# Output projection of a decoder trunk: a longer lag for the residual's squares and stores, and transfers of computed data issued from GpSimd's queue

## The chip, the cores and the metric

The kernel runs on one core of a Trainium2 chip. The metric is the device time of one execution in microseconds (us), lower is better. The core has four engines with instruction queues of their own, each worked off in order: TensorE (PE, matrix products into PSUM), VectorE (DVE, here V), ScalarE (ACT, here S) and GpSimd (POOL, here G). A fifth, SyncE (SP, `nc.sync`), issues transfers only. Transfers between the core's SBUF and device memory are issued from a queue, here SP's or POOL's, and run on 16 DMA engines. An instruction that waits holds up everything behind it in its queue.

## The reference: what is computed

One decoder layer over 2048 tokens of width 1024, all in float32. Two token mixers (a gated delta rule and a linear recurrence, four heads each) make `mix`. The part around the change is

```python
mix_out = jnp.einsum('btc,cd->btd', mix, w_out[i])
h = h + rms_norm(mix_out, post_mix_norm[i])

u = jnp.einsum('btd,df->btf', rms_norm(h, pre_mlp_norm[i]), w_mlp_up[i])
y = jnp.einsum('btf,fd->btd', jnp.square(jax.nn.relu(u)), w_mlp_down[i])
h = h + rms_norm(y, post_mlp_norm[i])
```

Behind it a per-layer embedding, projected and gated by a sigmoid, is added.

## The kernel before

**Stages.** Activations are held transposed: 128 channels on the partitions, 512 tokens (a block, `q` = 0 to 3) along a row. A 1024-wide activation of a block is eight tiles of 128x512 (256 KB each). The stages run one behind the other: input projection and token mixers (to about 1136 us), output projection (to about 1326 us), MLP up and down, gate. Every float32 operand of a product is split into a high part (ScalarE, L164 or L217) and a low part (VectorE, L165 or L218, which subtracts the high part and so follows ScalarE's half), and a product is three matmuls: high by high, high by low, low by high. PE needs a weight tile's high part first and its low part two matmuls later.

**Output projection (L1335 to L1382).** The loop goes over `j` = 0 to 31, that is four blocks `q` by eight output tiles `d`; one `(q, d)` is 24 matmuls, `mmo`. Its weights `w_out` are loaded raw (512 KB, L338) and split for the first three blocks, and reloaded as stored split (1 MB, L185) for the fourth, two or three tiles ahead. Three split weight buffers and two raw ones exist. ScalarE copies the result from PSUM (`yo`, L1374) and squares it (`sq_o`, L233); VectorE sums the squares (`acc_o`, L234).

For blocks 0 and 1 the sum goes through a norm (`rstd_steps`: split `hl`, product with ones on PE, L1156 and L1157, then logarithm, exponential and a correction on ScalarE and VectorE, to `r_o`). `residual_by_dma` then takes the eight tiles: VectorE scales one (L1210), POOL issues a transfer that adds x onto it in place (L1211), and some steps later its square goes into a second sum (`sq_h`, `acc_h`) and the tile is stored (`h1d`, L1214). From `acc_h` a second norm gives `rn`, the scale of the MLP's input.

For blocks 2 and 3 the unscaled tile is stored (`yod`, L1378) from a pool of two buffers, `stg`: the copy of tile d waits until the store of tile d - 2 has landed. Their residual is made later, within the MLP (`passed`).

**The MLP's operands.** The MLP's products are Strassen-like: seven products of sums of quarters. For the first half (blocks 0 and 1) `early_operands` reloads block 0's `h1d` as `be` (L1269), and `up_operands` reloads block 1's as `b` (L1288), in four steps of two tiles; VectorE scales them by `rn`, forms differences (L1293 to L1304) and splits them into `t`. Four quarter tiles of `w_up` are loaded into the raw buffers (`u_raw`, L1350), combined and split into `w_u`. PE's first products `u` (L1125) use `t` and `w_u`.

**What sets the order.** PE's order is as written. A clock ticks once every eight matmuls (`mm`, `tick`), and `later` puts the steps of a generator at tick offsets, here `OUT_STEPS`: one step of the residual per tick from offset 7 on, the second norm's product at offset 26. Within that, a planner decides how the instructions of ScalarE, VectorE, POOL and SP stand in their queues, and all of them run in that order. `pair` and `squares` rotate the buffers of the squares.

Of the kernel before, what the change touches and what calls it, by code (L numbers as in the profile page):

```python
# [43 lines left out]
N_CONST = C_MASK + len(LEVELS)  # L44


OUT_STEPS = (1, 5) + tuple(range(7, 18)) + (18, 26)
MLP_STEPS = (1, 5) + tuple(range(7, 25, 2))
AMID_STEPS = (1, 5) + tuple(range(12, 39, 3))

# [38 lines left out]
def trunk(ctx, tc, x, xT, pT, vecs, w_in, w_ab, gdn_a_log, gdn_dt_bias, w_out, w_up, w_down,  # L89
          w_ple, w_gate, consts, out):  # L90
    nc = tc.nc
    V, S, G, PE = nc.vector, nc.scalar, nc.gpsimd, nc.tensor
# [32 lines left out]
    def col(r):  # L125
        return cols[:, r : r + 1]
# [95 lines left out]
    def squares(acc, src, k, name, eng=V):  # L222

        if acc is None:
            acc = st.tile([P, QT], F32, tag="acc", name=f"acc_{name}", bufs=3)
            S.activation(acc, src, AF.Square)
        else:
            turns[0] += 1
            if pair[0] and turns[0] % 2:
                sq = st.tile([P, QT], F32, tag="late", name=f"sq_{name}_{k}")  # L230
            else:
                sq = st.tile([P, QT], F32, tag="sq", name=f"sq_{name}_{k}", bufs=1)
            S.activation(sq, src, AF.Square)  # L233
            eng.tensor_tensor(acc, acc, sq, ALU.add)  # L234
        return acc
# [23 lines left out]
    h1d = [[dr.tile([P, QT], F32, name=f"h1d{q}_{k}") for k in range(KD)] for q in range(NQ)]  # L259
# [63 lines left out]
    def mix_operands(q):  # L323
        xin[q] = []
        for k in range(KD):
            t = next_pool().tile([P, 2, QT], F32R, tag="ring", name=f"mixT{q}_{k}")
            nc.sync.dma_start(plain(t), mixd[q][k])
            split_in_place(t)
            xin[q].append(t)
            yield  # L330
# [4 lines left out]
    def stage_out(j):  # L335
        if j < len(order) and order[j][0] < RAW:
            raw = wp.tile([P, KD, P], F32, tag="raw", name=f"raw_out{j}", bufs=2)
            nc.sync.dma_start(raw, w_out[order[j][1]])  # L338
            staged_out[j] = raw
# [77 lines left out]
    with mixers as mctx:  # L417
# [515 lines left out]
        for q in range(NQ):  # L933
            works.append((f"ab{q}", "ab", w_ab, q, None, None, None, None))
            for h in range(4):
                g, b = {}, {}
# [97 lines left out]
        with tc.manual_schedule(engines={mybir.EngineType.SP}):  # L1034
# [26 lines left out]
            qs = (2, 3)  # L1061
# [25 lines left out]
            while clock[0] <= last or len(held) < 2 or 1 in ready:  # L1087
                if fill:
                    q, d = fill.pop(0)
# [26 lines left out]
    def later(gen, offsets):  # L1116
        for o in offsets:
            agenda.setdefault(clock[0] + o, []).append(gen)
# [21 lines left out]
    def ytile(name):  # L1140
        return f2.tile([P, QT], F32, tag="y", name=name, bufs=16)
# [61 lines left out]

    def residual_by_dma(q, ys, rsb, skip, gain, dst, name, sums):

        total, lag = None, 3
        for d in range(KD + lag):
            yield
            if d < KD:
                V.scalar_tensor_tensor(ys[d], ys[d], col(gain + d), rsb, ALU.mult, ALU.mult)  # L1210
                G.dma_start(ys[d], skip(d), accum_op=ALU.add)  # L1211
            if d >= lag:
                total = squares(total, ys[d - lag], d - lag, f"{sums}{q}")
                nc.sync.dma_start(dst[d - lag], ys[d - lag])  # L1214
        yield
        return total

# [26 lines left out]
    yod = {q: [dr.tile([P, QT], F32, name=f"yod{q}_{d}") for d in range(KD)] for q in (2, 3)}  # L1244

    def run(gen):
        for _ in gen:
            pass
# [4 lines left out]
    def moving(half, n, k, raw):  # L1253
        x = next_pool().tile([P, 2, QT], F32R, tag="ring", name=f"t{n}_{half}_{k}")
        split(x, V, raw)
        tops[half][n].append(x)

    def start_operands(half):
        tops[half] = {n: [] for n in ("11", "3", "1", "2", "21", "4", "22")}
# [3 lines left out]
    def early_operands():  # L1263

        start_operands(0)
        for k in range(KD // 2):
            for n, kk in (("11", k), ("21", k + KD // 2)):
                b = first_b[kk] = ytile(f"be_{kk}")
                nc.sync.dma_start(b, h1d[0][kk])  # L1269
                V.scalar_tensor_tensor(b, b, col(R_PREMLP + kk), h1_r[0], ALU.mult, ALU.mult)  # L1270
                moving(0, n, k, b)
                yield

    def up_operands(half, rsb):

        qs = (2 * half, 2 * half + 1)
        early = half in tops
        if not early:
            start_operands(half)
        for k in range(KD // 2):  # L1280
            n = f"{half}_{k}"
            b11, b21, b12, b22, t3, t2, t4 = (once(lambda i=i: ytile(f"b{i}_{n}")) for i in range(7))
            if early:
                b11, b21 = (lambda k=k: first_b[k]), (lambda k=k: first_b[k + KD // 2])
            for b, s, kk in ((b12, 1, k), (b22, 1, k + KD // 2), (b11, 0, k), (b21, 0, k + KD // 2)):
                if early and s == 0:
                    continue
                nc.sync.dma_start(b(), h1d[qs[s]][kk])  # L1288
                V.scalar_tensor_tensor(b(), b(), col(R_PREMLP + kk), rsb[s], ALU.mult, ALU.mult)
            yield  # L1290
            if not early:
                moving(half, "11", k, b11())
            V.tensor_tensor(t3(), b22(), b12(), ALU.subtract)  # L1293
            V.tensor_tensor(b12(), b12(), b11(), ALU.subtract)
            yield
            moving(half, "3", k, t3())
            moving(half, "1", k, b12())
            yield
            V.tensor_tensor(t2(), b22(), b12(), ALU.subtract)
            moving(half, "2", k, t2())  # L1300
            if not early:
                moving(half, "21", k, b21())
            yield
            V.tensor_tensor(t4(), b21(), t2(), ALU.subtract)  # L1304
            moving(half, "4", k, t4())
            moving(half, "22", k, b22())
            yield

    def once(make):
        kept = []  # L1310

        def get():
            if not kept:
                kept.append(make())
            return kept[0]

        return get
# [18 lines left out]
    for j, (q, d) in enumerate(order):  # L1336
        if d == 0:
            ys, acc = [], None
            if q < 2:
                later(mix_operands(q + 1), range(2, 18, 2))  # L1340
            if q == 1:
                later(mix_operands(3), range(17, 25))
        ready_out(j + 2)
        stage_out(j + 3)
        if j == len(order) - 5:
            u_raw = [wp.tile([P, 2, QT], F32, tag="raw", name=f"u_raw{i}", bufs=2) for i in range(2)]
            a1, a2 = w_up[0], w_up[FF // P // 2]
            for t, i, src in ((u_raw[0], 0, a1[:, : KD // 2]), (u_raw[1], 1, a1[:, KD // 2 :]),
                              (u_raw[0], 1, a2[:, : KD // 2]), (u_raw[1], 0, a2[:, KD // 2 :])):
                nc.sync.dma_start(t[:, i].rearrange("p (k n) -> p k n", n=P), src)  # L1350
        if j == len(order) - 2:
            two_blocks(("11", u_raw[0][:, 0]), ("12", u_raw[1][:, 1]))
        if j == len(order) - 1:
            (a11, a21), (s1, s4) = ((t[:, 0], t[:, 1]) for t in u_raw)
            b22 = two_blocks(("22", s1), None)
            V.tensor_tensor(s1, s1, a21, ALU.add)
            V.tensor_tensor(a21, a11, a21, ALU.subtract)
            V.tensor_tensor(a11, s1, a11, ALU.subtract)
            V.tensor_tensor(s4, s4, a11, ALU.subtract)
            u_block("3", b22, a21)  # L1360
        if (q, d) == (2, 1):
            early = early_operands()
            later(early, range(0, 2 * KD, 2))
        if prep is None and h1_r[1] is not None:
            run(early)
            prep = up_operands(0, h1_r)
            later(prep, range(0, 24, 1))
        if j in held:
            ps = held.pop(j)
        else:  # L1370
            ps = bank(f"mmo_{q}_{d}", pp)
            product(ps, columns(ready.pop(j)), xin[q])
        y = ytile(f"yo{q}_{d}") if q < 2 else tp.tile([P, QT], F32, tag="stg", name=f"yo{q}_{d}")
        S.activation(y, ps, AF.Copy)  # L1374
        acc = squares(acc, ps, d, f"o{q}")
        ys.append(y)
        if q >= 2:
            nc.sync.dma_start(yod[q][d], y)  # L1378
        if d == KD - 1 and q < 2:
            later(normed(q, ys, acc, lambda d, q=q: xT[blk(d), tok(q)], R_POSTMIX, h1d[q], "o", "h"), OUT_STEPS)  # L1380
        elif d == KD - 1:
            later(rstd_steps(acc, 1.0 / D, EPS, f"o{q}", row_of(o_r, q), po, wait=True), OUT_STEPS[:2] + (9,))  # L1382
    u_block("2", two_blocks(("1", s1), None), a11)
# [353 lines left out]
    for half in range(2):  # L1737
        qs = (2 * half, 2 * half + 1)
# [75 lines left out]
```

## Time and profile before

| | us |
|---|---|
| median of three runs | 2731.33 (2723.95 to 2732.11) |
| profiled execution | 2734.69 |
| its span | 2732.5 |
| PE busy | 2661.9 (97%) |
| VectorE busy | 2037.9 (75%) |
| ScalarE busy | 1467.6 (54%) |
| POOL busy | 116.7 (4%) |

A group of the page gives line, engine, operation, output and inputs, the count, then busy time and the mean of one in ns, then the idle time just ahead of it and who ended it. A row of the timeline gives the start, the length, the engine, line and operation, and the count where several follow each other; what stands in brackets is the idle time ahead of it and its releaser. `SPq` is SP's queue. A row of the waits gives who waited for whom, in total, how often, and the longest. The time of a transfer to its landing counts from its issue to the event that says that all its data are there.

### The profile page before, as it was taken

The page shows a single profiled execution, that of the slowest core. Times are in us where ns is not written, and L with a number is a line of the kernel's source. Part 1 is how long each engine was busy: PE and PEld are TensorE (multiplying, and loading weights), DVE is VectorE, ACT ScalarE, POOL GpSimd, SP SyncE. Part 2 cuts the span into 40 slices and gives each one's busy share as a digit, 9 for nine tenths or more (in the row PEclk, how much of TensorE's full clock was granted, in tenths as well). Part 3 has the DMA queues.
Part 4 walks back from the last instruction along what each step waited for, and adds up shares of the span by engine and source line. Part 5 has one row for each costly group of instructions (what it writes and reads, how often), then busy time and mean ns, then how long its engine had stood idle before and what let it go on. Part 6 is the DMA issues. An engine that isn't in the chain of part 4 may idle for free.

```text
span 2732.5 us, 38474 instructions
## 1 busy us (share of the span) xinstructions
PE 2661.9 (97%) x12745; PEld 2214.0 (81%) x12745; DVE 2037.9 (75%) x4228; ACT 1467.6 (54%) x2944; POOL 116.7 (4%) x120
## 2 busy tenths in 40 slices
PE   7999999999999999998999999999999999999999
PEld 5788788888888887776788888888888888888887
DVE  6788877787778777566889867767787765567776
ACT  6665555465546445566655646555554445465431
POOL 0000000000000000011000000001000000001000
PEclk9999999999999999999999999999999999999999
DMA  7777777667665665788566547667554446687664
GB/s 249 259 265 227 238 253 248 219 214 260 214 215 205 216 210 176 246 266 264 173 232 224 189 153 256 207 207 241 169 204 146 151 167 214 189 257 239 217 209 138
DMA packets 268742, 589.24 MB, mean 216 GB/s; under 512 B 55658, under 2 KB 60232, under 8 KB 249344
## 3 DMA queue, kind: packets, MB, share of 16 engines
q1 hardware_dynamic: 266240, 582.59, 64.3%
q0 software_dynamic: 2304, 4.20, 0.9%
q8 instruction: 101, 1.65, 0.3%
q14 instruction: 97, 0.79, 0.1%
HBM read 419.75 MB, written 166.92 MB: 215 GB/s over the span
## 4 chain that ended last, share of the span: by engine, by line
PE 51%; DMA 4%; issue 3%; DVE 2%; ACT 1%; POOL 1%; SPq 0%; DVEq 0%; POOLq 0%; ACTq 0%
PE u L1125 22%; PE d L1125 21%; PE mmg L1125 6%; PE mmo L1125 1%; DMA raw_out<-in_w_out_dram 1%; DMA yo<-in_xT_dram 1%; DMA b<-h1d 0%; POOL acc_y L234 0%; DMA mixT<-mixd 0%; DMA rd_g<-m_g 0%; DMA w_out<-cache_out 0%; PE mme L191 0%; DMA raw_pT<-in_pT_dram 0%; DVE t L165 0%; DMA m_g<-sd_g 0%
## 5 line engine op out<-in xcount | busy, mean ns | idle before, releaser
L1054 PE MATMUL mm<-xt,w 128*128 128x512 f32 x3072 | 784.9, 401 | 2.1 <-ACT zt_zg L559 2.1
L1054 PEld LDWEIGHTS mm<-xt,w 128*128 128x128 f32 x3072 | 554.3, 189 | 102.6 <-ACT zt_zg L559 2.5
L1125 PE MATMUL d<-db,da 128*128 128x512 f32 x2688 | 610.6, 389 | 0.2 <-DVE db L218 0.2
L1125 PE MATMUL u<-t,wu 128*128 128x512 f32 x2604 | 591.1, 389 | 0.0
L1125 PEld LDWEIGHTS d<-db,da 128*128 128x128 f32 x2688 | 504.5, 188 | 105.7 <-DVE db L218 1.0
L1125 PEld LDWEIGHTS u<-t,wu 128*128 128x128 f32 x2604 | 488.9, 188 | 101.4
L218 DVE TENSOR_TENSOR db<-db 128x512 fp32r<-128x512 f32 x224 | 160.0, 714 | 69.2 <-ACT db L217 68.2
L1477 DVE TENSOR_TENSOR u<-u,u 128x512 f32<-128x512 f32 x224 | 150.4, 683 | 57.2 <-PE u L1125 55.7
L1125 PE MATMUL mmo<-mixT,w_out 128*128 128x512 f32 x720 | 173.4, 400 | 14.8 <-ACT w_out L164 7.7
L217 ACT ACTIVATE db<-db 128x512 fp32r<-128x512 f32 x224 | 140.9, 629 | 74.8 <-DMA db<-hid 70.7
L1125 PEld LDWEIGHTS mmo<-mixT,w_out 128*128 128x128 f32 x720 | 137.5, 193 | 49.5 <-ACT w_out L164 10.4
L1125 PE MATMUL mmg<-h2T,wg 128*128 128x512 f32 (+1 forms) x792 | 174.8, 383 | 0.0
L1125 PEld LDWEIGHTS mmg<-h2T,wg 128*128 128x128 f32 x792 | 145.6, 188 | 29.0
L1520 ACT ACTIVATE u<-u 128x512 f32<-128x512 f32 x128 | 80.8, 631 | 161.3 <-DVE u L1477 160.8
L165 DVE TENSOR_TENSOR da<-da 128x512 fp32r<-128x512 f32 x128 | 93.6, 731 | 83.3 <-ACT da L164 83.0
L164 ACT ACTIVATE da<-da 128x512 fp32r<-128x512 f32 x128 | 80.5, 629 | 128.5 <-DMA da<-sumd 105.7
L164 ACT ACTIVATE wu<-a 128x512 fp32r<-128x512 f32 x124 | 75.0, 623 | 48.0 <-DMA a<-in_w_up_dram 46.1
L680 DVE TENSOR_TENSOR pr_g<-xs_g,sys_g 128x16 f32<-128x16 f32 (+14 forms) x240 | 94.4, 393 | 5.6
L165 DVE TENSOR_TENSOR wu<-a,wu 128x512 fp32r<-128x512 f32 x124 | 85.7, 693 | 10.5 <-ACT wu L164 10.5
L234 POOL TENSOR_TENSOR acc_y<-acc_y,sq_y 128x512 f32<-128x512 f32 x28 | 38.6, 1380 | 1253.7 <-ACT sq_y L233 1253.7
L1521 ACT ACTIVATE u<-u 128x512 f32<-128x512 f32 x128 | 80.5, 629 | 3.1
L165 DVE TENSOR_TENSOR da<-dr,da 128x512 fp32r<-128x512 f32 x96 | 66.3, 691 | 18.0 <-ACT da L164 16.0
(383 smaller groups left out, 3790.9 us busy)
## 6 DMA issues: line engine op xcount, KB each, us to landing
w<-cache_in SPq DMA_DIRECT2D x96, 1024.0 KB
db<-hid SPq DMA_DIRECT2D x224, 256.0 KB
cache_in<-w SPq DMA_DIRECT2D x32, 1024.0 KB
hid<-u SPq DMA_DIRECT2D x128, 256.0 KB
da<-sumd SPq DMA_DIRECT2D x128, 256.0 KB
a<-in_w_up_dram SPq DMA_DIRECT2D x124, 256.0 KB
hid<-ht SPq DMA_DIRECT2D x96, 256.0 KB
dr<-in_w_down_dram SPq DMA_DIRECT2D x96, 256.0 KB
```

The lines of the kernel that those rows point to most:

```text
L164: S.activation(t[:, 0], raw, AF.Copy)
L165: eng.tensor_tensor(t[:, 1], raw, t[:, 0], ALU.subtract)
L217: S.activation(t[:, 0], plain(t), AF.Copy)
L218: V.tensor_tensor(t[:, 1], plain(t), t[:, 0], ALU.subtract)
L234: eng.tensor_tensor(acc, acc, sq, ALU.add)
L680: V.tensor_tensor(pr[:, :, :, 0:i], xs[:, None, :, 0:i].broadcast_to([P, 2, GC, i]), sys[:, 0:i, i : i + 2].rearrange("p j two -> p two j" ...
L1054: PE.matmul(ps, *terms[i], start=i == 0, stop=i == nt - 1)
L1125: PE.matmul(ps, a, b, start=start, stop=stop)
L1477: V.tensor_tensor(c[new], c[old], ps, ALU.add)
L1520: S.activation(c[k], c[k], AF.Relu)
L1521: S.activation(c[k], c[k], AF.Square)
```

## The change

The lag between a tile's scaling and its square and store in `residual_by_dma` goes from three steps to five, and `OUT_STEPS` gets two more steps in the row so that the generator ends at the same tick (26); the split of the summed squares moves from offset 18 to 20. The stores `h1d` of blocks 0 and 1, the stores `yod` of blocks 2 and 3, the reloads `be`, and the loads `b` of the MLP's first half are issued from POOL's queue instead of SP's. These are the transfers of the stage that wait for computed data. Loads of weights and of `mixT` stay on SP.

```diff
-OUT_STEPS = (1, 5) + tuple(range(7, 18)) + (18, 26)
+OUT_STEPS = (1, 5) + tuple(range(7, 20)) + (20, 26)
...
     def residual_by_dma(q, ys, rsb, skip, gain, dst, name, sums):
 
-        total, lag = None, 3
+        total, lag = None, 5
         for d in range(KD + lag):
             yield
             if d < KD:
                 V.scalar_tensor_tensor(ys[d], ys[d], col(gain + d), rsb, ALU.mult, ALU.mult)
                 G.dma_start(ys[d], skip(d), accum_op=ALU.add)
             if d >= lag:
                 total = squares(total, ys[d - lag], d - lag, f"{sums}{q}")
-                nc.sync.dma_start(dst[d - lag], ys[d - lag])
+                G.dma_start(dst[d - lag], ys[d - lag])
...
                 b = first_b[kk] = ytile(f"be_{kk}")
-                nc.sync.dma_start(b, h1d[0][kk])
+                G.dma_start(b, h1d[0][kk])
...
-                nc.sync.dma_start(b(), h1d[qs[s]][kk])
+                (nc.sync if half else G).dma_start(b(), h1d[qs[s]][kk])
...
         if q >= 2:
-            nc.sync.dma_start(yod[q][d], y)
+            G.dma_start(yod[q][d], y)
```

## The prediction

> **What bounds the kernel now.** The page comes first: its span, and the groups of TensorE by line.
>
> ```profile
> span 2732.5 us, 38474 instructions
> ...
> L1125 PE MATMUL u<-t,wu 128*128 128x512 f32 x2604 | 591.1, 389 | 0.0
> ...
> L1125 PE MATMUL mmo<-mixT,w_out 128*128 128x512 f32 x720 | 173.4, 400 | 14.8 <-ACT w_out L164 7.7
> ```
>
> PE sets the time. In the MLP's first product (`u`) it never idles; in the output projection (`mmo`), the stage of the change, it idles 14.8 us, mostly for weights that ScalarE and VectorE split. A microsecond saved here counts only if the next stage takes it over. The timeline of PE shows where it stops (a bracket is the idle time before the row, and who ended it).
>
> ```profile
> 1186.88 34.62 PE L1125 MATMUL mmo<-mixT,w_out 128*128 128x512 f32 x152
> 1222.31 0.73 PE L1125 MATMUL mmo<-mixT,w_out 128*128 128x512 f32 x2 [0.82 <-ACT w_out L164]
> 1223.57 3.47 PE L1125 MATMUL mmo<-mixT,w_out 128*128 128x512 f32 x14 [0.53 <-DVE w_out L165]
> ...
> 1248.35 11.83 PE L1125 MATMUL mmo<-mixT,w_out 128*128 128x512 f32 x48 [0.53 <-DVE w_out L165]
> 1261.14 5.29 PE L1125 MATMUL mmo<-mixT,w_out 128*128 128x512 f32 x22 [0.96 <-DVE w_out L165]
> 1268.71 0.79 PE L1125 MATMUL mmo<-mixT,w_out 128*128 128x512 f32 x2 [2.29 <-ACT w_out L164]
> 1271.70 7.34 PE L1125 MATMUL mmo<-mixT,w_out 128*128 128x512 f32 x22 [2.19 <-DVE w_out L165]
> 1281.12 3.96 PE L1125 MATMUL mmo<-mixT,w_out 128*128 128x512 f32 x16 [2.08 <-DMA w_out<-cache_out]
> ...
> 1291.27 34.62 PE L1125 MATMUL mmo<-mixT,w_out 128*128 128x512 f32 x152
> ...
> 1331.91 0.73 PE L1125 MATMUL u<-t,w_u 128*128 128x512 f32 x2 [0.58 <-ACT w_u L164]
> 1333.05 2.11 PE L1125 MATMUL u<-t,w_u 128*128 128x512 f32 x8 [0.41 <-DVE w_u L165]
> ```
>
> Undisturbed, matmuls follow each other by (34.62 - 0.39) / 151 = 0.227 us (row 1291.27). By that pace the first block would reach the third row at 1221.8; it starts at 1223.57: 1.8 us lost. In the same way 1.9 are lost ahead of 1261.14, 2.6 ahead of 1268.71, 2.5 ahead of 1271.70 and 4.4 ahead of 1281.12: 13.2 us in all, which is the most that this change can win here. The last two rows matter as much: behind the stage PE already waits, if briefly, for VectorE and ScalarE. PE has no lead there to give away.
>
> Why are the weights late? The waits of the stretch 1185 to 1335, of the engines and of SP's queue:
>
> ```profile
> ACT sq_h L233 <- DMA yo<-in_xT_dram: 16.0, 11, 2.5
> ```
> ```profile
> SPq L1214 <- DMA yo<-in_xT_dram: 34.3, 13, 7.0
> ```
>
> Both wait for the accumulating transfer that adds x onto the scaled tile (L1211). ScalarE's squares come three ticks (of eight matmuls, 1.8 us) behind the scaling, the transfer is often not in, and the split of the weights stands behind the square. SP's store waits likewise, with weight loads queued behind it. ScalarE's timeline:
>
> ```profile
> 1220.20 0.63 ACT L233 ACTIVATE sq_h<-yo 128x512 f32<-128x512 f32 x1 [2.44 <-DMA yo<-in_xT_dram]
> ...
> 1221.21 1.05 ACT L164 ACTIVATE w_out<-raw_out 128x1024 fp32r<-128x1024 f32 x1
> ...
> 1255.08 0.63 ACT L226 ACTIVATE acc_h<-yo 128x512 f32<-128x512 f32 x1 [3.67 <-DMA yo<-in_xT_dram]
> ...
> 1262.12 0.63 ACT L233 ACTIVATE sq_h<-yo 128x512 f32<-128x512 f32 x1 [2.10 <-DMA yo<-in_xT_dram]
> 1264.44 0.63 ACT L233 ACTIVATE sq_h<-yo 128x512 f32<-128x512 f32 x1 [1.68 <-DMA yo<-in_xT_dram]
> ...
> 1267.62 1.04 ACT L164 ACTIVATE w_out<-raw_out 128x1024 fp32r<-128x1024 f32 x1
> ...
> 1274.02 0.63 ACT L233 ACTIVATE sq_h<-yo 128x512 f32<-128x512 f32 x1 [1.72 <-DMA yo<-in_xT_dram]
> ...
> 1282.47 0.60 ACT L1374 ACTIVATE yo<-mmo 128x512 f32<-128x512 f32 x1 [4.33 <-DMA yod<-yo]
> ...
> 1285.58 0.63 ACT L164 ACTIVATE hl_o<-acc_o 128x512 fp32r<-128x512 f32 x1 [2.02 <-PE nrm_h L1157]
> ```
>
> **The change, part by part.** No arithmetic is added or removed, and PE's order stays as it is. Two more ticks (3.6 us) put squares and stores later; `OUT_STEPS` is stretched so that the sum's split comes two ticks later and the norm at the same tick 26. 48 issues (16 stores `h1d`, 16 stores `yod`, 8 loads `be`, 8 loads `b`) leave SP for POOL, which now has only the 16 adds there. POOL's rows, and VectorE's and SP's that the steps need:
>
> ```profile
> 1251.39 0.88 POOL L1211 DMA_DIRECT2D yo<-in_xT_dram  x1 [37.84 <-DVE yo L1210]
> ...
> 1255.06 2.68 POOL L1211 DMA_DIRECT2D yo<-in_xT_dram  x3 [1.52 <-DVE yo L1210]
> 1262.64 0.88 POOL L1211 DMA_DIRECT2D yo<-in_xT_dram  x1 [4.90 <-DVE yo L1210]
> ...
> 1267.41 0.88 POOL L1211 DMA_DIRECT2D yo<-in_xT_dram  x1 [2.10 <-DVE yo L1210]
> ```
> ```profile
> L1211 POOL DMA_DIRECT2D yo<-in_xT_dram x16: 875/875/1355, 1198.3 to 1267.4; - x16
> ...
> DMA to landing us min/median/max: 3.7/6.4/10.6
> ```
> ```profile
> 1270.43 1.22 DVE L165 TENSOR_TENSOR w_out<-raw_out,w_out 128x1024 fp32r<-128x1024 f32 x1
> ...
> 1304.89 1.42 DVE L1289 SCALAR_TENSOR_TENSOR b<-b,cols,rn 128x512 f32<-128x512 f32 x2 [0.82 <-DMA b<-h1d]
> ...
> 1315.80 0.75 DVE L1289 SCALAR_TENSOR_TENSOR b<-b,cols,rn 128x512 f32<-128x512 f32 x1 [0.65 <-DMA b<-h1d]
> ...
> 1322.30 1.42 DVE L1289 SCALAR_TENSOR_TENSOR b<-b,cols,rn 128x512 f32<-128x512 f32 x2
> ```
> ```profile
> 1273.27 0.47 SPq L185 DMA_DIRECT2D w_out<-cache_out  x1
> ...
> 1274.37 0.40 SPq L1378 DMA_DIRECT2D yod<-yo  x1
> ...
> 1300.20 0.92 SPq L1288 DMA_DIRECT2D b<-h1d  x2
> ...
> 1319.60 0.88 SPq L1288 DMA_DIRECT2D b<-h1d  x2
> ```
>
> *First block (q = 0).* ScalarE's order in the changed program has the split of 1221.21 ahead of the last two squares, behind the sixth, which can run at about 1216.6 as its data land. The split starts near 1218, before PE asks: the 1.8 us go. VectorE's queue, which takes over the waits in between, comes out 1.4 us earlier. I take 1.4.
>
> *Second block (q = 1).* The changed POOL queue reads:
>
> ```
> add0 add1 store0 add2 add3 add4 yod3 store1 store2 store3 add5 add6 yod4 add7 store4 .. store7 yod5 b b yod6 yod7
> ```
>
> A store waits until its add has landed, and the adds behind it wait too. Store0 goes at 1255.08 (add0 has landed), so adds 2 to 4 go 0.9 later than now. Store2 waits for add2: now 1255.06 to 1262.12, 7.1 us; so 1263.0. Store3 waits for add3: 8.5 from its issue to 1264.44; so 1265.4. Add5 then goes at 1266.2 in place of 1262.64, add7 at 1268.9 in place of 1267.41. The two ticks of lag are thus eaten by a new wait on POOL; what remains is the order on ScalarE: the split of 1267.62 no longer stands behind the fourth square, only behind the third (1263.0), a copy and a square of PSUM: 1264.6. VectorE's half now ends at 1271.65; behind three short operations it would end at 1268.7. PE's block at 1271.70 moves by 3.0 us. The reload of 1273.27 stands on SP behind two loads that wait for that split; with no store between, it goes 1.2 behind the split rather than 1.6: 1269.9. With the 7.8 us to its use now (1273.27 to 1281.12) it is in at 1277.7: 3.4 us won. Together PE reaches 1281.12's block 1.4 + 3.4 = 4.8 us earlier.
>
> *What is late next.* The first MLP products need operands made from `rn` (second block) and the `b` loads, by a chain on VectorE that is nearly gapless until the `w_u` that PE waits for at 1333.05. `rn` stands on ScalarE behind the copy of 1282.47, which waits for the store `yod5`. That store, now issued at 1274.37 and in 8.1 us later, would stand on POOL behind store7, which waits for add7 (6.6 us, 1267.41 to 1274.02): 1276.4, less the 1.4 above. With the adds' median of 6.4 the copy runs at 1281.4, 1.1 earlier; the wait of 1285.58 behind it, 1.3 of which was for PE, goes as well: `rn` comes 2.4 earlier, not 4.8.
>
> *Loads of `b`.* Three pairs are loaded just in time (1304.89 and 1315.80 wait for them already). Today the pair of 1319.60 is used by 1322.30: at most 2.7 us, issues of 0.44. On POOL an issue takes 0.875, and no plain transfer there is in the trace: the nearest row is the adds' minimum of 3.7. Each pair is 0.4 + 1.0 = 1.4 later, 4.2 for three. Bounds: nothing (the first pair of four is hidden by `rn`, and the others' waits could stay as they are), and the adds' maximum of 10.6, which gives 8.3 for the third pair and 6.3 for each of the two that now take some 4.7 (1300.20 to 1304.89): 21. I stay near the low end, because an add also reads its target.
>
> *The other issues.* The `be` loads start behind store7 at some 1222, not at 1228.68 as on SP, and wait for `rn` of the first block; nothing. If POOL's issues all took the 1.355 seen once, the 24 of one block cost 12 us of a queue that mostly waits; nothing on the path. `w_u` for PE's wait at 1331.91 stands three VectorE operations (1.8 us) later in the new order; 0.84 us of waits for the norm behind it absorb part, and most of the rest is three splits done earlier: 0.3.
>
> *The clock.* PE would reach that wait 4.8 us early and be served about 2 late: some 7 us of idle time at a stretch. What that does to the granted clock, the table of windows shows (columns: stretch, length, then busy time and count of PE, PEld, DVE, ACT, POOL, then clock, DMA share, GB/s):
>
> ```profile
> 1272.00:1276.00 4.00, 4.00 (x10) 3.13 (x10) 2.97 (x6) 1.97 (x4) 0.00 (x0) 0.50 1.06 372
> ```
>
> After the stops of 2.29 and 2.19 the clock is 0.50 and 22 matmuls take 7.34 instead of 5.2: 2.1 us. I book 2.5, between that and nothing lost (a wait for the norm hides it) or the same again. The Trainium skill, page "TensorE: Matmul & The Clock Gate", section "Part 1: The HAM clock gate", has the clock halve after about 3.4 us of idleness and return after as much busy time: an estimate of 1.7 us per stop from that page, where the row gives 2.1; by it the sum would be 0.8 lower, with the same verdict.
>
> *Sum.* -2.4 + 4.2 + 0.3 + 2.5 = +4.6 us. From there on PE runs without idle time and carries the difference to the end. The profiled execution took 2734.7 (span 2732.5), so 2739; the median of the three runs, 3.4 below it, becomes 2731.3 + 4.6, near 2736. The stall goes, and its gain is given back one stage later. The DMA share in that last row, 1.06, says besides that moving issues between queues makes no room for bytes.
>
> **The rivals.** *Gain kept (faster).* If plain transfers on POOL land in about 2.7 us and store2 and store3 no longer hold the adds, all 13.2 us go, and the operand chain must move with them: 2718. For it: every stop listed leads back to the squares or to SP's queue. Against: `rn` behind yod5, and a VectorE chain with hardly a gap.
>
> *Half kept.* Loads hidden, 4.8 us stay won: 2726.5. Against it are the `b` waits that exist already.
>
> *Late loads (slower).* One mechanism: plain transfers on POOL's queue land like its adds do under load. With 6.4 for the third pair (+4.1) and 10.6 for the two beside the 1 MB reloads (+6.3 each) it is 16.7 in place of 4.2, in all +17: 2748; the bound of 21 gives 2753. It decides, by 0.3%, when a pair costs over 2.6 us. For it: median 6.4 against SP's 2.7; the queue of 64 in one line. Against: the adds move more. The Trainium skill, page "DMA: Bandwidth & Descriptors", section "Issuing engine by pattern", gives simple loads and stores to Sync and calls that path generally faster. So far the trace leans the same way, 2.7 against 3.7 at best.
>
> *No effect at all*: lag and queue change what VectorE and ScalarE run next, but the reload and `rn` are where they were: 2731.
>
> **How the numbers follow.** 0.3%, 8.2 us, is about what a measurement of this kernel tells from no change; the three runs lie as far apart (2723.95 to 2732.11). Chances: given back (2729 to 2739) 0.38, no effect 0.07, half kept 0.10, all kept 0.13, late loads 0.32. Faster 0.13, same 0.55, slower 0.32. The range runs from the faster rival to the slower one's bound, 2719 to 2753; the likeliest case alone is 2729 to 2739.
>
> **What would show it.** The squares' waits for the adds nearly gone from ScalarE, and as waits of stores on POOL instead; PE's stops at 1222 gone, those at 1261 to 1281 shorter by some 3 us in sum; PE idle about 7 us in `u` behind the stage, with a dip of the clock; `b` waits on VectorE of 2 us each. I am wrong if PE's stops go and `u` doesn't wait, or if `b` or `yod` transfers take over 7 us.

## The result and the profile after

The changed kernel takes 2737.84 us (median of 16 runs, 2733.02 to 2742.26), the kernel before 2731.2 (16 runs beside them). The ratio is 1.0025, with a 95% interval of 1.0018 to 1.0032: slower by 4.9 to 8.7 us, 6.6 at the middle. Predicted were 2736, and as the likeliest outcome a time within 0.3% of the kernel before.

The page of the changed kernel, its span and PE's group in the output projection:

```profile
span 2735.1 us, 38478 instructions
L1125 PE MATMUL mmo<-mixT,w_out 128*128 128x512 f32 x720 | 170.0, 396 | 13.6 <-DMA w_out<-cache_out 4.8
```

PE's idle time in the stage fell only from 14.8 to 13.6 us, and its largest part now waits for a transfer, no longer for ScalarE's split. PE's timeline, first of the changed kernel:

```profile
1182.49 0.39 PE L1156 MATMUL nrm_o<-hl_o,ones 128*128 128x512 f32 x1
...
1262.70 6.88 PE L1125 MATMUL mmo<-mixT,w_out 128*128 128x512 f32 x22 [1.96 <-DVE w_out L165]
1274.38 5.50 PE L1125 MATMUL mmo<-mixT,w_out 128*128 128x512 f32 x16 [4.80 <-DMA w_out<-cache_out]
1286.07 18.30 PE L1125 MATMUL mmo<-mixT,w_out 128*128 128x512 f32 x80
1306.35 16.60 PE L1125 MATMUL mmo<-mixT,w_out 128*128 128x512 f32 x72 [1.99 <-ACT t L164]
1322.79 5.60 PE L1125 MATMUL u<-t,w_u 128*128 128x512 f32 x24
1332.74 7.08 PE L1125 MATMUL u<-t,w_u 128*128 128x512 f32 x16 [4.35 <-ACT w_u L164]
1340.11 10.16 PE L1125 MATMUL u<-t,w_u 128*128 128x512 f32 x44
```

And three rows of the kernel before that the prediction did not need:

```profile
1186.42 0.39 PE L1156 MATMUL nrm_o<-hl_o,ones 128*128 128x512 f32 x1
...
1325.72 5.60 PE L1125 MATMUL u<-t,w_u 128*128 128x512 f32 x24
...
1338.21 10.15 PE L1125 MATMUL u<-t,w_u 128*128 128x512 f32 x44
```

The first row of each is the product of the sums for the norm `o` of the first block. Up to there the two traces differ by 3.93 us, though the instructions stand in the same order in both, so all that follows is counted from this row, and differences are after minus before.

| place | before | after | difference |
|---|---|---|---|
| block of 22 matmuls behind the stops of the splits | 85.28 | 80.21 | -5.07 |
| block that waits for the reload | 94.70 | 91.89 | -2.81 |
| the block behind it (1291.27, 1286.07) | 104.85 | 103.58 | -1.27 |
| first product `u` | 139.30 | 140.30 | +1.00 |
| the product that waits for ScalarE's half of `w_u` | 145.49 | 150.25 | +4.76 |
| the 44 products of `u` behind it | 151.79 | 157.62 | +5.83 |

The gain is there, 5.1 us at its best, and is gone before the projection ends. From the last row on PE runs in both (2732.5 - 1338.21 = 1394.3 to the end before, 2735.1 - 1340.11 = 1395.0 after). So the +5.83 of this stretch is what the runs measure as 6.6.

The waits of the changed kernel in this stretch, the first for a store on POOL's queue:

```profile
POOL h1d L1214 <- DMA yo<-in_xT_dram: 24.2, 12, 4.1
ACT sq_h L233 <- DMA yo<-in_xT_dram: 19.1, 8, 4.7
...
DVE b L1289 <- DMA b<-h1d: 5.2, 2, 4.7
```

The squares do not wait less than before (16.0), they wait more: the stores hold the adds behind them on POOL, and the two ticks of lag are used up. `b` on VectorE (2.1 us in three waits before) appears with one long wait. POOL, VectorE, ScalarE and SP's queue of the changed kernel where it matters:

```profile
1267.11 0.57 POOL L1214 DMA_DIRECT2D h1d<-yo  x1 [4.11 <-DMA yo<-in_xT_dram]
...
1270.94 0.54 POOL L1378 DMA_DIRECT2D yod<-yo  x1
...
1304.64 0.54 POOL L1378 DMA_DIRECT2D yod<-yo  x1 [4.82 <-ACT yo L1374]
1305.17 1.09 POOL L1288 DMA_DIRECT2D b<-h1d  x2
```
```profile
1287.92 0.69 DVE L1166 TENSOR_TENSOR rn<-rn,rr_h 128x512 f32<-128x512 f32 x1
...
1299.83 1.43 DVE L1289 SCALAR_TENSOR_TENSOR b<-b,cols,rn 128x512 f32<-128x512 f32 x2 [0.16 <-issue]
...
1312.80 0.75 DVE L1289 SCALAR_TENSOR_TENSOR b<-b,cols,rn 128x512 f32<-128x512 f32 x1 [4.73 <-DMA b<-h1d]
1314.02 0.75 DVE L1289 SCALAR_TENSOR_TENSOR b<-b,cols,rn 128x512 f32<-128x512 f32 x1 [0.47 <-DMA b<-h1d]
...
1321.09 1.41 DVE L1289 SCALAR_TENSOR_TENSOR b<-b,cols,rn 128x512 f32<-128x512 f32 x2
```
```profile
1279.27 0.60 ACT L1374 ACTIVATE yo<-mmo 128x512 f32<-128x512 f32 x1 [4.11 <-DMA yod<-yo]
...
1330.86 0.63 ACT L164 ACTIVATE w_u<-u_raw 128x512 fp32r<-128x512 f32 x1 [3.23 <-DVE u_raw L1356]
```
```profile
1263.09 2.07 SPq L185 DMA_DIRECT2D w_out<-cache_out  x1
...
1297.89 0.24 SPq L1177 DMA_DIRECT2D row<-r_o  x1
1298.23 1.05 SPq L185 DMA_DIRECT2D w_out<-cache_out  x2
...
1304.40 0.32 SPq L185 DMA_DIRECT2D w_out<-cache_out  x1
```

The same pair in the kernel before, on SP's queue and on VectorE:

```profile
1309.41 0.32 SPq L1378 DMA_DIRECT2D yod<-yo  x1
1309.79 0.91 SPq L1288 DMA_DIRECT2D b<-h1d  x2
1310.80 0.38 SPq L185 DMA_DIRECT2D w_out<-cache_out  x1
```
```profile
1313.81 0.75 DVE L1289 SCALAR_TENSOR_TENSOR b<-b,cols,rn 128x512 f32<-128x512 f32 x1 [0.69 <-DMA b<-h1d]
```

In both kernels this pair is issued right behind a `yod` store, and at the same place (1309.79 - 1186.42 = 123.37 before, 1305.17 - 1182.49 = 122.68 after). What differs is how long it takes: its first half is used 4.0 us after the issue before, 7.6 after. On SP the reload of 1 MB stood behind `yod` and `b` and followed them by 1.0 us (1310.80); with those gone from its queue it goes out 0.77 us ahead of the pair (1304.40). VectorE's chain then carries the lateness to ScalarE's half of `w_u` (the ACT row of 1330.86 waits for VectorE; the one that releases PE follows it at 1332.06), for which PE stops 4.35 us.

### The profile page after: what moved, and what is told of

Same layout as the page of the kernel before. It is cut to its first block, busy times and chain, and to the rows that moved or that the text cites. A ratio compares the mean times of both kernels' runs of the same rounds, so it can differ in the third digit from the quotient of the medians.

```text
span 2735.1 us, 38478 instructions
## 1 busy us (share of the span) xinstructions
PE 2659.0 (97%) x12745; PEld 2213.1 (81%) x12745; DVE 2036.4 (74%) x4228; ACT 1466.6 (54%) x2944; POOL 143.0 (5%) x168
## 4 chain that ended last, share of the span: by engine, by line
PE 51%; DMA 5%; DVE 3%; ACT 2%; issue 1%; POOL 1%; SPq 0%; POOLq 0%; DVEq 0%; ACTq 0%
PE u L1125 22%; PE d L1125 22%; PE mmg L1125 6%; DMA yo<-in_xT_dram 1%; DMA raw_out<-in_w_out_dram 1%; DMA b<-h1d 0%; PE mmo L1125 0%; POOL acc_y L234 0%; DMA mixT<-mixd 0%; DMA yod<-yo 0%; DMA rd_g<-m_g 0%; DVE t L165 0%; DMA raw_pT<-in_pT_dram 0%; DMA m_g<-sd_g 0%; DMA dr<-in_w_down_dram 0%
## 5 line engine op out<-in xcount | busy, mean ns | idle before, releaser
L1125 PE MATMUL mmo<-mixT,w_out 128*128 128x512 f32 x720 | 170.0, 396 | 13.6 <-DMA w_out<-cache_out 4.8
```

Of the source, the lines that this page charges most:

```text
L1125: PE.matmul(ps, a, b, start=start, stop=stop)
```

## The experiments

The theory of the prediction is: the projection's gain is given back in the first products `u`, whose operands come by a VectorE chain that `rn` and the `b` loads set. The rivals: a loss that lies in the projection itself (stores that hold the adds), and plain transfers on POOL that are slow as such. With the profile after in hand the theory got a sharper form (Theory A in the later expectations): the second pair is late because it stands behind `yod` on POOL and lands beside the reloads, not because of POOL's path itself. All diffs are against the changed kernel; ratios are to the kernel before, run on the same chip.

**Lag alone**: five ticks, all transfers on SP.

```diff
-                G.dma_start(dst[d - lag], ys[d - lag])
+                nc.sync.dma_start(dst[d - lag], ys[d - lag])
... (and the other three issues of the change likewise)
```

> Only the lag (five ticks) and OUT_STEPS; every transfer stays on SP. My theory: the adds are no longer held by stores, so the squares' waits for them (22 us in sum before) all but go and PE reaches the MLP some 6 us earlier; VectorE's operand chain starts with rn, perhaps 3 us earlier, and the b loads are as quick as before. Ratio to before 0.999 (2728.5), and PE's waits in the first MLP products grow from 1.0 to some 4 us. Rival (the later squares themselves cost): rn comes 3.6 us later and the time is +2 us or more (1.001).

Measured: 2731.14 us, ratio 1.0003 (0.9994 to 1.0011).

```profile
1276.98 6.53 PE L1125 MATMUL mmo<-mixT,w_out 128*128 128x512 f32 x16 [8.38 <-DMA w_out<-cache_out]
```

The squares' waits fall (11.0 us instead of 16.0), and still nothing is won: PE waits 8.38 us for the reload. `u` waits only 0.17, not the 4 us expected, and the 0.999 expected lies outside the interval. So the lag by itself turns one stop into another, and the loss in `u` needs the queue.

**Queue alone**: lag 3 and the old `OUT_STEPS`, transfers on POOL.

```diff
-        total, lag = None, 5
+        total, lag = None, 3
```

> Only the queue; lag three as before. My theory: POOL's stores hold the adds while the squares come as early as before, so ScalarE waits longer for the adds (30 us and more in place of 22), PE's stops in the projection stay or grow, and the late b loads are added: +8 to +12 us, ratio 1.0035. Rival (the queue costs nothing, what costs is the lag): ratio 1.000.

Measured: 2740.25 us, ratio 1.0038 (1.0025 to 1.0052), as expected. The squares wait 22.4 us (16.0 before), `b` 4.8, `u` 5.08. The queue is the slower part. That the longer lag gives some of it back is likely, but the intervals of the two kernels (1.0018 to 1.0032 with it) overlap.

**`b` back on SP**, the rest as changed:

```diff
-                (nc.sync if half else G).dma_start(b(), h1d[qs[s]][kk])
+                nc.sync.dma_start(b(), h1d[qs[s]][kk])
```

> The changed kernel with the b loads back on SP. My theory: the 4.7 us wait of VectorE for the second pair of b shrinks to about 1, the operands are ready some 3.5 us earlier: 2734, ratio 1.001 to before. Rival (the loads are not what the end waits for): as the changed kernel, 1.0025.

Measured: 2727.56 us, ratio 0.9988 (0.9979 to 0.9996). Eight loads are worth some 10 us of the changed kernel, more than expected. SP's queue and VectorE:

```profile
1302.44 1.08 SPq L1288 DMA_DIRECT2D b<-h1d  x2
```
```profile
1311.12 1.41 DVE L1289 SCALAR_TENSOR_TENSOR b<-b,cols,rn 128x512 f32<-128x512 f32 x2
```

The pair goes out 3.7 us earlier (1302.44 - 1183.50 = 118.94 from the norm's row, against 1305.17 - 1182.49 = 122.68), and VectorE has no `b` wait at all. The squares still wait 22.8 us and the stores on POOL 27.3: these waits, far longer than those for `b` had been, cost little at the end.

**`h1d` stores back on SP**, the rest as changed:

```diff
-                G.dma_start(dst[d - lag], ys[d - lag])
+                nc.sync.dma_start(dst[d - lag], ys[d - lag])
```

> The changed kernel with the h1d stores back on SP, lag five. My theory: adds 2 to 7 go as soon as their tile is scaled, the squares' waits fall from 24 to under 10 us, yod5 is not behind store7, rn comes 2 to 3 us earlier: 2735, ratio 1.0015; the b loads on POOL remain and keep it above before. Rival (stores on SP block the reloads again, as before the change): PE's stops of the second block are back and the ratio is 1.0025 or more.

Measured: 2735.27 us, ratio 1.0022 (1.0013 to 1.003). The squares' waits fall from 19.1 to 11.4, the `b` wait stays at 5.3, `u` waits 4.71, and the time is that of the changed kernel within the intervals. This speaks against the rival that the loss lies in the stores that hold the adds. It does not settle it alone, since the stores stand ahead of the reloads again and PE's stop for the reload grows to 6.54 us (4.80 in the changed kernel); and the interval holds both the 1.0015 of the theory and the 1.0025 of its rival.

**`yod` stores back on SP**, `b` stays on POOL:

```diff
-            G.dma_start(yod[q][d], y)
+            nc.sync.dma_start(yod[q][d], y)
```

> The changed kernel with the yod stores back on SP; adds, h1d, be and b stay on POOL. The b loads then have no yod store ahead of them on POOL, and the reloads on SP are spaced by the yod stores as before. Theory A (the second pair of b is late because it stands behind yod3 and because SP, freed of stores, lets 3 MB of reloads out in one go beside it): VectorE's wait for the pair falls from 5.2 us to under 2, ratio 1.001. Theory B (a plain load issued from POOL lands in 7 to 8 us by itself): the wait stays at 4 us or more, ratio 1.0025.

Measured: 2723.14 us, ratio 0.9996 (0.9987 to 1.0004). POOL's queue and VectorE:

```profile
1291.24 0.55 POOL L1288 DMA_DIRECT2D b<-h1d  x1 [14.53 <-DVE t L165]
1292.44 0.55 POOL L1288 DMA_DIRECT2D b<-h1d  x1 [0.66 <-DVE b L1304]
```
```profile
1303.55 1.41 DVE L1289 SCALAR_TENSOR_TENSOR b<-b,cols,rn 128x512 f32<-128x512 f32 x2
```

With no `yod` store in front, the pair is issued as soon as its buffers are free, 7.4 us earlier from the norm's row (1291.24 - 1175.92 = 115.32), still on POOL, and no `b` wait is left. A plain load on POOL's queue is early enough when nothing holds it. The edit also puts stores between the reloads on SP again (the reloads go out at 1294.05, 1296.10 and 1301.54), so it does not tell the two halves of Theory A apart.

**Without the last two reloads.** One execution; which weights the last two tiles use instead stands in the expectation.

```diff
-        ready_out(j + 2)
+        if j + 2 < len(order) - 2:
+            ready_out(j + 2)
...
-            product(ps, columns(ready.pop(j)), xin[q])
+            product(ps, columns(ready[min(j, len(order) - 3)]), xin[q])
```

> The changed kernel without the last two reloads of w_out (tiles 30 and 31 of the projection use tile 29's weights, so their output is another one): 2 MB less traffic beside the second pair of b. What is read is that pair's time from issue to use. Theory A (collision with the reloads): it falls from 8 us to 4 or 5. Theory B (POOL's path itself): 7 us or more. The total is not compared, since the planner's order of the combinations of w_up changes with it.

Measured: 2723.24 us, beside 2723.67 of the kernel before (one run against a median, so no ratio). POOL and VectorE:

```profile
1298.49 1.09 POOL L1288 DMA_DIRECT2D b<-h1d  x2
```
```profile
1303.02 1.43 DVE L1289 SCALAR_TENSOR_TENSOR b<-b,cols,rn 128x512 f32<-128x512 f32 x2 [1.04 <-DMA b<-h1d]
```

The pair is issued at the same place as in the changed kernel (1298.49 - 1176.03 = 122.46 against 122.68), and its first half is used 4.5 us later instead of 7.6. The table of windows shows the transfer engines while the pair flies, for the changed kernel and for this one (the last two columns are DMA share and GB/s):

```profile
1309.00:1311.00 2.00, 2.00 (x10) 1.66 (x9) 0.00 (x0) 0.49 (x2) 1.62 (x3) 1.00 1.00 414
```
```profile
1298.00:1300.00 2.00, 0.00 (x0) 0.02 (x1) 2.00 (x4) 2.00 (x5) 1.58 (x3) 0.96 0.60 234
```

The share alone says little: in the next two stretches of this kernel it is 0.86 and 0.88, at 199 and 212 GB/s. The landing says more: without 2 MB of reloads 3.1 us of it go, from the same queue, if in a single execution. The two experiments before show that an earlier issue covers the slow landing.

Traces of further kernels below tell queue and reloads apart, for the same second pair. With the `row` stores on POOL it is issued from POOL, behind a `yod` store, 6.5 us after the last reload (1306.89), and is used 3.9 us later. With the stores on ScalarE it is issued from SP, 0.4 us behind a reload (1291.41), and takes 6.8 us, 2.11 of which VectorE waits:

```profile
1313.42 1.10 POOL L1288 DMA_DIRECT2D b<-h1d  x2
```
```profile
1291.82 0.86 SPq L1288 DMA_DIRECT2D b<-h1d  x2
```
```profile
1298.66 0.75 DVE L1289 SCALAR_TENSOR_TENSOR b<-b,cols,rn 128x512 f32<-128x512 f32 x1 [2.11 <-DMA b<-h1d]
```

So clear of reloads the pair lands in 3.9 to 4.5 us from POOL and, ahead of the reload, in 4.0 from SP; right behind or beside them it takes 6.8 from SP and 7.6 from POOL (other traces of this section: 5.5 from SP, 7.3 to 8.2 from POOL). The reloads make the pair late from either queue. What POOL's queue adds beside them, somewhere between nothing and 2.7 us, is not settled.

**Operand steps earlier**: the generator that makes the operands spreads over 17 ticks instead of 24.

```diff
-            later(prep, range(0, 24, 1))
+            later(prep, range(0, 17, 1))
```

> The changed kernel with seven fewer ticks in the schedule of the operands (17 in place of 24), which in the planner's order puts the combinations of w_up ahead of the last operand splits on VectorE. Theory (PE's 4.4 us wait in the first MLP products is for w_u, last in VectorE's queue): the wait falls by 1.5 to 2 us and so does the time: ratio 1.0018 to 1.002. Rival (PE then waits for the operands t instead): 1.0025.

Measured: 2727.24 us, ratio 1.0013 (1.0004 to 1.0022). `u` waits 2.86 + 0.41 instead of 4.35, a fall of 1.1 where 1.5 to 2 were expected; the `b` wait stays (5.3), and a longer stop in the projection is the price:

```profile
1300.79 18.20 PE L1125 MATMUL mmo<-mixT,w_out 128*128 128x512 f32 x72 [4.15 <-ACT t L164]
```

**`row` stores on POOL.** The stop at 1306.35 in the changed kernel was not foreseen; a reload stood on SP behind the small store of 1297.89, which had waited for `r_o`.

```profile
SPq L1177 <- DVE r_o L1166: 9.4, 1, 9.4
```
```diff
-            nc.sync.dma_start(rows[q], r[0:1, :])
+            G.dma_start(rows[q], r[0:1, :])
```

> The changed kernel with the small stores `row` (L1177) on GpSimd's queue in place of SyncE's, where one waits 9.4 us for `r_o` with a reload of `w_out` behind it (1288.5 to 1297.89). Theory L (the stop of 1306, 1.99, is the reload that comes too late): the reload is issued near 1289, the stop goes, the three reloads no longer start together at 1298, and the second pair of `b` lands sooner: its wait of 4.73 falls below 2. Ratio to the kernel before 1.000 to 1.001. Theory S (the stop is ScalarE's order of splits and the late pair is GpSimd's queue alone): stop and `b` wait stay within 1 us of what they are, ratio 1.0025.

Measured: 2737.22 us, ratio 1.0020 (1.0009 to 1.0031): the time did not move. The trace says why:

```profile
1324.56 5.28 PE L1125 MATMUL u<-t,w_u 128*128 128x512 f32 x22 [0.94 <-DVE w_u L165]
1336.67 5.75 PE L1125 MATMUL u<-t,w_u 128*128 128x512 f32 x16 [6.83 <-ACT w_u L164]
```
```profile
1293.53 0.69 DVE L1166 TENSOR_TENSOR rn<-rn,rr_h 128x512 f32<-128x512 f32 x1
...
1308.07 1.43 DVE L1289 SCALAR_TENSOR_TENSOR b<-b,cols,rn 128x512 f32<-128x512 f32 x2 [2.80 <-issue]
...
1317.30 1.42 DVE L1289 SCALAR_TENSOR_TENSOR b<-b,cols,rn 128x512 f32<-128x512 f32 x2 [0.99 <-DMA b<-h1d]
```

Theory L was half right. The stop of 1306 is gone and the first `u` starts 1.27 earlier (1323.01 - 1183.98 = 139.03 against 140.30); the second pair's wait is 0.99 where it was 5.2. But the first pair now waits 2.80 (the profile names no releaser; its loads were issued 6.2 us before its use), `rn` itself came 4.1 later in this execution (109.55 from the norm's row against 105.43), and PE waits 6.83 for `w_u`. A microsecond that PE wins in the projection buys a microsecond of waiting in `u`: the chain behind `rn` sets the time. The 4.1 us are hardly the edit's, since the store it moves is issued behind `rn`: on POOL the last `h1d` store, which waits for its add, goes out 4.4 us later (1276.34 - 1183.98 = 92.36 against 1270.41 - 1182.49 = 87.92), and `yod` and `rn` follow. Whether that varies from run to run was not measured; in the trace of `b` on SP the store goes out at 91.65.

**Stores on ScalarE's queue**, behind the square or copy that precedes them; loads `be` and `b` on SP; lag 5.

```diff
-                G.dma_start(dst[d - lag], ys[d - lag])
+                S.dma_start(dst[d - lag], ys[d - lag])
...
-                G.dma_start(b, h1d[0][kk])
+                nc.sync.dma_start(b, h1d[0][kk])
...
-                (nc.sync if half else G).dma_start(b(), h1d[qs[s]][kk])
+                nc.sync.dma_start(b(), h1d[qs[s]][kk])
...
-            G.dma_start(yod[q][d], y)
+            S.dma_start(yod[q][d], y)
```

> Lag five; the h1d and yod stores issued from ScalarE's queue, right behind the square or copy that has already waited for the data, be and b from SP. Nothing on POOL holds the adds, nothing on SP holds the reloads, and the loads are quick. If an issue costs ScalarE little (under 0.1 us), all stops but those at 1243 go and the ratio is 0.997 (2723); if it costs as much as on SP (0.32 to 0.44 us, 32 of them, some 12 us of ScalarE in a stage where it has slack), 0.999. Rival: ScalarE becomes the bound and it is over 1.001.

Measured: 2718.89 us beside 2723.67, ratio 0.9978 (0.9969 to 0.9987): faster than both kernels. PE's stops that are left in the projection's second half, and the issues:

```profile
1260.41 5.30 PE L1125 MATMUL mmo<-mixT,w_out 128*128 128x512 f32 x16 [4.22 <-DMA w_out<-cache_out]
...
1271.93 6.30 PE L1125 MATMUL mmo<-mixT,w_out 128*128 128x512 f32 x16 [3.95 <-DMA w_out<-cache_out]
...
1319.35 3.47 PE L1125 MATMUL u<-t,w_u 128*128 128x512 f32 x14 [0.30 <-DVE w_u L165]
```
```profile
L1214 ACTq DMA_DIRECT2D h1d<-yo x16: 326/326/348, 1191.1 to 1262.7; - x16
```

This is the kernel of "lag alone" (1.0003) with only the stores on another queue. Two stops for reloads are left (4.22 and 3.95), against the expectation, and the squares wait longer for the adds (23.4 us) than in either kernel. A store there waits for nothing that ScalarE has not waited for already, it holds no add on POOL and no load on SP, and costs 0.33 us of issue. **The same with the `row` stores on POOL**:

> The kernel with lag 5, stores of `h1d` and `yod` on ScalarE's queue and `be` and `b` on SyncE's, now with the `row` stores on GpSimd's. It has no stop at the place of 1306 and no `b` waits, only two waits for reloads (4.22 and 3.95), of which the second's reload is issued before the `row` store. Theory L: nothing to win there, ratio 0.997 to 0.999, same as without the edit. Rival: the reload behind the `row` store was about to be late, or the earlier reloads crowd others out: ratio differs by over 0.001 from 0.9978.

Measured: 2725.87 us beside 2731.32, ratio 0.9977 (0.9967 to 0.9988), the same as without. There was no stop at that place to win. (Its expectation speaks of no `b` waits in the kernel without the edit; there were 2.4 us of them.)

Beside each other, counted from the norm's row as in the table above (the kernel before: 139.30 and 151.79), which shows where each version loses:

| kernel | ratio | first `u` | the 44 products | PE's wait for `w_u` |
|---|---|---|---|---|
| changed | 1.0025 | +1.00 | +5.83 | 4.35 |
| lag alone | 1.0003 | +1.53 | +0.41 | 0.17 |
| queue alone | 1.0038 | +4.36 | +8.40 | 5.08 |
| `b` on SP | 0.9988 | +0.46 | -0.09 | 1.87 |
| `h1d` on SP | 1.0022 | -0.48 | +3.43 | 4.87 |
| `yod` on SP | 0.9996 | +2.55 | +0.16 | 0.24 |
| steps earlier | 1.0013 | +4.80 | +7.19 | 3.27 |
| `row` on POOL | 1.0020 | -0.27 | +6.94 | 0.94 + 6.83 |
| stores on ScalarE | 0.9978 | -1.30 | -3.66 | 0.30 |
| the same, `row` on POOL | 0.9977 | -1.70 | -4.67 | none |

The fourth column goes with the ratio, the third hardly: `h1d` on SP and `row` on POOL reach `u` earlier than the kernel before and are slower. The traces are single executions: the 44 products of several rows lie 2 to 4 us off what the ratio gives, "steps earlier" by most (+7.19, where 1.0013 is 3.5 us), so nothing is read from that row's place in the order.

## Why the prediction was right, and where its steps were not

The time (2736 predicted, 2737.84 measured) and the path held: the chain of `rn`, the `b` loads and VectorE sets the time, and PE waits for it in `u`. How the gain is lost did not: in the prediction PE arrives 4.8 us early at `u` and gives that back there, but the gain was gone before, in the projection, and PE arrives 1.0 late. The sum of +4.6 came out as +5.83 in the trace, from terms that were mis-sized in both directions, so that the sum lands so near is partly luck:

| step | predicted | measured |
|---|---|---|
| first block's stop | -1.4 | -0.65 |
| splits ahead of the fourth square (block of 22) | -4.4 (1.4 + 3.0) | -5.07 |
| reload's block | -4.8 | -2.81 |
| `rn` | -2.4 | -0.48 |
| three `b` pairs | +4.2 (1.4 each) | +3.20 (-0.65, +3.28, +0.57) |
| `w_u` order | +0.3 | +2.04 |
| clock behind PE's wait | +2.5 | +1.07 |
| sum of the last four | +4.6 | +5.83 |

*First block.* The stop of 1222 went, as foreseen. Part of its 1.8 us came back as PE's waits for the splits `hl_h` (0.57) and `hl_o` (0.30), which the step did not look at.

*POOL's queue, replayed.* Right: stores wait for adds there (24.2 us, 12 times). The inference for ScalarE, that the squares' waits would be nearly gone, was wrong, and contradicted the replay that stood above it: adds held on POOL land later, and the squares wait 19.1 us. That this costs little at the end is the likely reading of two runs: with `h1d` on SP they wait 11.4 and the time stays, with the stores on ScalarE they wait 23.4 and the time is the lowest of all.

*The reload.* It was issued earlier, as foreseen (1263.09, 80.60 from the norm's row, 6.25 earlier than before). The step that failed is the 7.8 us to its use, taken over from the trace of before: it took 1274.38 - 1263.09 = 11.3. In the lag-only kernel as well PE waits 8.38 there. That the bytes beside it are the cause is argued from a DMA share of 0.98 to 1.11 between 1263 and 1274, not shown.

*Behind it* the clock was not counted. PE's 16 matmuls after the stop of 4.80 take 5.50 us where the pace of 0.227 gives 15 x 0.227 + 0.39 = 3.8, at a granted clock of 0.55 from 1274 to 1277. The 1.7 us lost fit the Trainium skill's page "TensorE: Matmul & The Clock Gate", section "Part 1: The HAM clock gate", by whose rule the prediction estimated 1.7 per stop. The stop of 4.35 in `u` does not fit it: the 16 matmuls behind it take 7.08 us, 3.3 over the pace.

*The stop of 1306* was in no step. `row` on POOL shows that it goes when the reload need not stand behind the `row` store, and that the time stays, since PE waits in `u` anyway.

*`rn`.* The copy of `yo` waits for `yod` as foreseen, 4.11 us, but the store was issued at 1270.94 and took 8.3 to land, on a queue where the median taken was 6.4. The order was right, the landing too short.

*The `b` pairs.* 1.4 each was the wrong shape. The first pair is hidden (its wait of 0.82 even goes), the second costs 3.28. The step that failed is the 1.0 us of longer landing, booked alike for each pair (3.7 for 2.7). The 2.7 was read from the third pair, which on POOL goes out 11.3 us before its use (1309.84) and does not wait; for the second it was 3.6 (7.6 for 4.0), and the eight loads on POOL took 3.5 / 7.2 / 10.0 us to land (least, median, most), mostly under cover. It asked how slow POOL's transfers are, and not what SP would send once `b` and `yod` no longer stood ahead of the reload in its queue. This is the slower rival's mechanism, late loads, with a price on one pair of three. The prediction named `b` or `yod` transfers of over 7 us as a sign against itself, and both came (7.6 for this pair, 8.3 for the `yod` above); the price of the pair was 3.3 where that rival had 6.3. The Trainium skill, page "DMA: Bandwidth & Descriptors", section "Issuing engine by pattern", puts plain loads on Sync: for `b` the runs agree (0.9988 against 1.0025). That POOL is slow for them as such they do not bear out: `yod` on SP is at 0.9996, and with `row` on POOL the pair lands in 3.9 us.

*`w_u` order.* Predicted 0.3 because "most of the rest is three splits done earlier". From the last pair's scaling to the wait's end it takes 11.65 us (1321.09 to 1332.74) against 9.61 (1322.30 to 1331.91). It is likely that the splits done earlier lay in the cover of the waits; the ones moved ahead of `w_u` lie on the path, and 2.04 is about the 1.8 that the prediction had before it discounted.

*The clock in `u`.* PE's wait was 4.35 us and not 7, since PE arrived 1.0 late and not 4.8 early. The dip came all the same; the table of windows (columns as in the prediction):

```profile
1334.00:1338.00 4.00, 4.00 (x10) 3.13 (x11) 4.00 (x8) 2.20 (x4) 0.00 (x0) 0.50 0.00 0
```

From the end of the wait to the 44 products it is 1340.11 - 1332.74 = 7.37 us against 6.30 before: +1.07, as before had its own waits for the norm there (0.84).

The rivals: the gain was not kept, in whole or in half, since `rn` came hardly earlier; no effect at all is ruled out by the interval (0.18% to 0.32%), which reaches just over the 0.3% that the prediction drew between "same" and "slower". The range's lower end, 2719, lies 1 us above the 2718 of the rival that it is said to start from.

## What to carry to other kernels

When a change frees an engine that is ahead of the bound, follow the chain that the next stage waits for before counting the gain: here (`row` on POOL) a microsecond won in the projection only lengthened the wait for `w_u`. A queue runs in order, so a load that must be early may not stand behind a store that waits for a result; put a store on the queue of the engine that makes the last wait anyway (here ScalarE, 0.33 us per issue, ratio 0.9978), and keep prefetches apart. A shared queue also keeps an order: when a load leaves it, the bulk transfer that stood behind it may go first.

## What was not expected of the hardware

A plain transfer of 256 KB costs POOL some 0.55 us of issue (`1305.17 1.09 POOL L1288`, for two), not the 0.875 of an accumulating one that the prediction used; on ScalarE's queue it is 0.33. Under load the time to land depended more on what flew beside it than on the queue: the second `b` pair took 7.6 us from POOL and 6.8 from SP beside the reloads, and 4.5 from POOL with 2 MB less. And long waits were not the dearest: the squares' waits could fall from 19.1 to 11.4 us without the time moving (`h1d` on SP), while taking away the 5.2 us of `b` waits won some 10 (`b` on SP).
